# Relative-bias tables read from short rows in reverse key order, the second table built after the first MLP, and two weight splits moved to VectorE

## The chip, the cores and the metric

The kernel runs on one core of one Trainium2 chip. The metric is the device time in microseconds of one execution of the whole program. Six instruction streams run side by side: TensorE (PE, with its weight loads shown as PEld), VectorE (DVE), ScalarE (ACT), GpSimd (POOL), and the queues from which transfers are issued; SyncE (SP) does nothing else, ACT and POOL issue some transfers between their computations. Each stream works its instructions in order.

## The reference, cut to what matters

A sequence of 256 tokens with 1024 features goes through a first block of two layers and a second block. All of it is float32; the kernel gets float32 accuracy by splitting each operand into a high part (rounded to the type that TensorE multiplies fast) and the rest, and by adding three products.

```
# first block, layer A: attention with an indexer and a relative bias
score = sum_h w[t,h] * relu(q_idx[t,h] . k_idx[s]) * ...   # top 64 keys of a token are kept
logits[h,t,s] = q[t,h].k[s] / 8 + rel_bias[bucket(s - t)][h]     # 16 heads, 32 buckets
h = h + softmax(logits) @ v @ a_w_o
h = h + relu(rms(h) @ up)**2 @ down                         # MLP 0
# layer B: latent attention, no bias table
h = h + mla(h) @ b_w_o ;  h = h + MLP 1
# second block: mLSTM beside attention in 3 groups of 8 heads
logits[g,h,t,s] = q.k / 8 + rel_bias_2[bucket(t - s)][8 g + h]   # masked outside the group's window
h = merge(...) ; h = h + gated FFN ; out = rms(h) * g
```

A bias depends only on the distance between key and query. For each head it is one row of some 383 numbers, and the 256 x 256 bias of a head is that row, shifted by one place from one query to the next.

## The kernel before, in words

Tokens lie on the 128 partitions in two tiles t = 0 and 1; the residual stream stays on the chip in `hres[0]` and `hres[1]`. Weights are streamed: `wsplit` loads up to four 128-row blocks into a tile `raw` (3 buffers) over SP's queue, ACT makes the high part `whi`, and DVE the rest `wlo` (4 buffers each). A load waits until the split of three loads earlier has read its buffer, and a split waits until TensorE has finished with the weights of four splits earlier.

The program is written with a tile framework that derives the waits and also reorders the instructions of each engine by a cost model of its own; the plans `PLAN_A`, `PLAN_B` and `PLAN_C` only give the order in which the pieces are handed to it. In `PLAN_A` "s" is the indexer's scores of a tile (`scores`), "k" its top-k (`topk`, eight rounds of maximum and replace on DVE, which end in the mask `madd`), "q" the query projection, "t" the transposes of the queries, a star a round of attention steps, and "x" the making of the second bias table.

A bias table is made in two steps. `bias_rows` multiplies a one-hot matrix `oh` (33 x 512, from the constant `c_oh`) by the table `rb` on TensorE into `bt`, ACT copies that to `bts`, and a transfer on ACT's queue writes the rows to `vec` in device memory. Then a second transfer on ACT's queue, device memory to device memory, writes for each head and each of 128 queries the shifted row of 256 keys: `toe_a` (16 heads, 2 MB) and `toe_b` (24 heads, 3 MB). `load_bias` reads four heads at a time from there over SP's queue. In `att_step` one DVE instruction for each head (CUSTOM_DVE_ANT in the profile, line 547) adds bias and logits and takes the maximum; ACT takes the exponential, TensorE transposes the result (`tr`), ACT or DVE copies it (`pT`, a pool of two buffers), and TensorE multiplies by the values into `po`.

The rest `wlo` of the second half of the columns of `a_w_o` and `b_w_o` (four instructions of 128x1024 each) is computed on POOL (`eng=G`), all others on DVE. At the end of MLP 0 the last chunks of the down projection (`dn`) are added to `hres`; layer B then takes sums of squares of `hres` (`sq`, ACT), transposes it (`tr`), splits the result (`bxh`, `bxl`) and multiplies it by `w_dkv` and `b_w_dq`, whose splits carry the gains `gckv` and `gcq`; `low_rank` scales the outcome into `lc`. The tables `tabk` and `tabq` of the rotary embedding are made on DVE from small loads (`rp`, `bgk`, `bgq`).

Of the kernel before, what the change touches and what calls it, by code (L numbers as in the profile page):

```python
# [17 lines left out]
P = 128  # L18
S = 256
# [8 lines left out]
PLAN_A = "s0 k0 q0 q1 t00 t01 s1 * t10 k1 *4 x t11 **"  # L28
# [7 lines left out]
def constants():  # L36
# [31 lines left out]
    c["c_oh"] = oh  # L68
# [21 lines left out]
def block_kernel(ctx: ExitStack, tc: tile.TileContext, a, out: bass.AP):  # L90
# [55 lines left out]
    nc.sync.dma_start(hres[0], a["x"][0, 0:P, :])  # L146
    nc.sync.dma_start(ident, a["c_sq"][:, 0:128])

# [88 lines left out]
    def wsplit(w, k0, kk, c0, n, gain=None, eng=None):  # L237
# [22 lines left out]
    def wparts(w, KT, c0, n, k0=0, gain=None, eng=None):  # L260
        return [(g, min(4, KT - g), wsplit(w, k0 + g, min(4, KT - g), c0, n, gain, eng)) for g in range(0, KT, 4)]
# [20 lines left out]
    def dense_by_tile(jobs, engs=(None, None), holds=(None, None)):  # L282

        parts = []
        for (_, KT, w, c0, n, gain, _), e, hold in zip(jobs, engs, holds):
            with behind(hold):
                parts.append(wparts(w, KT, c0, n, gain=gain, eng=e))
# [87 lines left out]
    def mlp(i):  # L375
# [36 lines left out]
        last([6, 7])  # L412

# [899 lines left out]
```

## Time and profile before

| | |
|---|---|
| three timed runs | 1178.22, 1170.07, 1175.39 us (median 1175.39) |
| the profiled execution | 1170.38 us, of which the span of the trace is 1168.6 us |
| busy in the span | PE 97%, weight loads 85%, DVE 58%, ACT 52%, POOL 9% |
| moved by transfers | 197.16 MB, 169 GB/s in the mean |
| chain that ended last | PE 87%, DVE 4%, DMA 3%, ACT 2%, POOL 2% |

The profiled execution is 5.0 us below the median of the timed runs and 0.3 us above the fastest. The busy shares are means over stages that differ: TensorE has hardly any idle time in the MLPs and the second block, and most of it in the two attention layers of the first block and at both ends.

### The profile page before, as it was taken

The numbers are of one execution on the slowest core, as the hardware profiler recorded it, in microseconds if no ns is written. First come the engines' busy times: TensorE is split into PE (matmuls) and PEld (weight loads), VectorE is DVE, ScalarE is ACT, GpSimd is POOL, SyncE is SP. The second block draws the span as 40 slices with busy tenths as digits, with TensorE's granted clock in tenths as the row PEclk, the third lists the DMA queues.
The fourth block names the chain that finished last, engine by engine and source line by source line (L and its number), as shares of the span: only waits on it lengthen the run. The fifth ranks groups of instructions, "written<-read, shape, count | busy, mean of one in ns | idle before, by whom it ended". The sixth has DMA issues, their size and how long they took to land.

```text
span 1168.6 us, 17282 instructions
## 1 busy us (share of the span) xinstructions
PE 1128.3 (97%) x6912; PEld 994.9 (85%) x6912; DVE 680.9 (58%) x1182; ACT 613.0 (52%) x1070; POOL 109.6 (9%) x128
## 2 busy tenths in 40 slices
PE   7979899999997999999999999999999999999997
PEld 6747799899886888998889999889888878999996
DVE  5694654544578666445446885655474556544544
ACT  7564555544577556455546574464564435443443
POOL 1250000000039400000000000010000030000000
PEclk9999999999999999999999999999999999999999
DMA  8954455555355226555626644553544544546541
GB/s 276 303 154 92 144 182 179 198 199 164 102 150 173 91 73 216 198 181 185 210 88 244 212 154 145 201 177 132 180 158 144 169 138 162 195 166 216 199 137 62
DMA packets 110339, 197.16 MB, mean 169 GB/s; under 512 B 6580, under 2 KB 28044, under 8 KB 110260
## 3 DMA queue, kind: packets, MB, share of 16 engines
q1 hardware_dynamic: 103704, 186.90, 47.7%
q10 hardware_dynamic: 5516, 5.64, 2.1%
q0 software_dynamic: 1040, 3.54, 1.1%
q8 instruction: 54, 0.88, 0.3%
q14 instruction: 25, 0.20, 0.1%
HBM read 194.93 MB, written 6.37 MB: 172 GB/s over the span
## 4 chain that ended last, share of the span: by engine, by line
PE 87%; DVE 4%; DMA 3%; ACT 2%; POOL 2%; issue 1%; SPq 0%; ACTq 0%; POOLq 0%; DVEq 0%
PE acc L269 8%; PE acc L270 8%; PE acc L272 8%; PE dn L356 7%; PE dn L355 7%; PE dn L358 7%; PE up L304 5%; PE up L307 5%; PE up L305 5%; PE tr L164 3%; PE po L503 3%; PE lg L479 2%; PE qk L305 2%; PE qk L304 2%; PE qk L307 2%; DMA toe_a<-vec 2%
## 5 line engine op out<-in xcount | busy, mean ns | idle before, releaser
L250 DVE TENSOR_TENSOR wlo<-raw,whi 128x1024 fp32r<-128x1024 f32 (+3 forms) x332 | 376.7, 1176 | 210.7 <-ACT whi L247 210.1
L247 ACT ACTIVATE whi<-raw 128x1024 fp32r<-128x1024 f32 (+3 forms) x340 | 323.2, 1008 | 212.4 <-PE dn L358 84.9
L157 POOL TENSOR_TENSOR rr<-rv,mhalf 128x1 f32<-128x1 f32 (+2 forms) x42 | 40.4, 961 | 796.3 <-DVE rv L155 794.0
L304 PE MATMUL up<-mxh,whi 128*128 128x256 f32 x448 | 111.5, 282 | 0.0
L305 PE MATMUL up<-mxl,whi 128*128 128x256 f32 x448 | 111.2, 280 | 0.0
L356 PE MATMUL dn<-wlo,uh 128*128 128x512 f32 x256 | 100.6, 394 | 0.0
L355 PE MATMUL dn<-whi,uh 128*128 128x512 f32 x256 | 100.2, 393 | 0.0
L304 PEld LDWEIGHTS up<-mxh,whi 128*128 128x128 f32 x448 | 84.3, 188 | 0.7
L305 PEld LDWEIGHTS up<-mxl,whi 128*128 128x128 f32 x448 | 84.3, 188 | 0.7
L269 PE MATMUL acc<-whi,cxh 128*128 128x512 f32 (+1 forms) x192 | 74.6, 390 | 0.0
L270 PE MATMUL acc<-wlo,cxh 128*128 128x512 f32 (+1 forms) x192 | 72.4, 378 | 0.0
L307 PE MATMUL up<-mxh,wlo 128*128 128x256 f32 x448 | 71.2, 281 | 0.0
L358 PE MATMUL dn<-whi,ul 128*128 128x512 f32 x256 | 69.6, 394 | 0.0
L307 PEld LDWEIGHTS up<-mxh,wlo 128*128 128x128 f32 x448 | 60.6, 188 | 0.0
L358 PEld LDWEIGHTS dn<-whi,ul 128*128 128x128 f32 x256 | 48.1, 188 | 11.2
L355 PEld LDWEIGHTS dn<-whi,uh 128*128 128x128 f32 x256 | 48.1, 188 | 10.6
L356 PEld LDWEIGHTS dn<-wlo,uh 128*128 128x128 f32 x256 | 48.1, 188 | 10.6
L272 PE MATMUL acc<-whi,cxl 128*128 128x512 f32 (+1 forms) x192 | 50.5, 382 | 0.0
L168 DVE TENSOR_TENSOR ul<-sq,uh 128x512 fp32r<-128x512 f32 x28 | 19.4, 692 | 51.2 <-ACT uh L168 50.8
L304 PE MATMUL qk<-cxh,whi 128*128 128x256 f32 x192 | 49.1, 287 | 0.0
L305 PE MATMUL qk<-cxl,whi 128*128 128x256 f32 x192 | 48.3, 282 | 0.0
L487 ACT ACTIVATE lg<-lg,nx 128x128 f32<-128x128 f32 (+1 forms) x80 | 35.5, 446 | 17.3 <-DVE nx L547 16.7
(414 smaller groups left out, 2461.6 us busy)
## 6 DMA issues: line engine op xcount, KB each, us to landing
raw<-in_w_in SPq DMA_DIRECT2D x38, 1024.0 KB
raw<-in_mlp_w_up SPq DMA_DIRECT2D x32, 1024.0 KB
raw<-in_mlp_w_down SPq DMA_DIRECT2D x32, 1024.0 KB
raw<-in_w_gate SPq DMA_DIRECT2D x10, 1024.0 KB
raw<-in_w_up SPq DMA_DIRECT2D x10, 1024.0 KB
raw<-in_w_down SPq DMA_DIRECT2D x10, 1024.0 KB
raw<-in_w_in SPq DMA_DIRECT2D x6, 688.0 KB
raw<-in_a_w_in SPq DMA_DIRECT2D x4, 1024.0 KB
```

Of the source, the lines that this page charges most:

```text
L157: G.tensor_tensor(r[:, :n], v[:, :n], mhalf[:, :n], op=OP.pow)
L247: A.activation(hi[:, c], raw[:, c], AF.Copy)
L250: (eng or V).tensor_tensor(lo[:, c], raw[:, c], hi[:, c].bitcast(F32), op=OP.subtract)
L269: PE.matmul(o, s0, wh[:, k, :], start=(g + k == 0), stop=False)
L270: PE.matmul(o, s0, wl[:, k, :], start=False, stop=False)
L272: PE.matmul(o, xs(xl, g + k, t), wh[:, k, :], start=False, stop=(g + k == KT - 1))
L304: PE.matmul(o, s0, xh[(g + k) // 4][:, (g + k) % 4, :], start=(g + k == 0), stop=False)
L305: PE.matmul(o, s0, xl[(g + k) // 4][:, (g + k) % 4, :], start=False, stop=False)
L307: PE.matmul(o, wl[:, k, col:col + P], xh[(g + k) // 4][:, (g + k) % 4, :], start=False, stop=(g + k == KT - 1))
L355: PE.matmul(ps, s0, wh[:, k, :], start=(c == 0 and k == 0), stop=False)
L356: PE.matmul(ps, s0, wl[:, k, :], start=False, stop=False)
L358: PE.matmul(ps, xs(u[1], k, t), wh[:, k, :], start=False, stop=(c == nc_ - 1 and k == kt - 1))
```

## The change

There are five edits. (1) The large tables `toe_a` and `toe_b` go away: the one-hot constant is stored with its key axis reversed, so that `load_bias` can read the shifted rows straight from `vec` (partition step +1, key step +1) and `att_step` reads the loaded tile backwards (`Sk - 1::-1`). (2) The second table is built at the end of MLP 0 (`biases_2`) instead of inside layer A ("x" leaves `PLAN_A`). (3) The one-hot tiles are loaded over SP's queue instead of ACT's, and take the buffers of `pT`; `bts` takes those of `sq`, and `bt` those of the transposes. (4) The first tile of `x` is loaded in two halves and the first weight group in four blocks. (5) The splits of `a_w_o` and `b_w_o` are all on DVE.

```diff
-PLAN_A = "s0 k0 q0 q1 t00 t01 s1 * t10 k1 *4 x t11 **"
+PLAN_A = "s0 k0 q0 q1 t00 t01 s1 * t10 k1 *4 t11 **"
...
-    c["c_oh"] = oh
+    c["c_oh"] = np.concatenate([oh[:, :, 382::-1], np.zeros((33, 4, 129), np.float32)], axis=2)
...
-    nc.sync.dma_start(hres[0], a["x"][0, 0:P, :])
+    nc.sync.dma_start(hres[0][:, 0:512], a["x"][0, 0:P, 0:512])
     nc.sync.dma_start(ident, a["c_sq"][:, 0:128])
+    nc.sync.dma_start(hres[0][:, 512:1024], a["x"][0, 0:P, 512:1024])
...
+        if by_k:
+            for k in range(kk):
+                nc.sync.dma_start(raw[:, k * n:(k + 1) * n], w[(k0 + k) * P:(k0 + k + 1) * P, c0:c0 + n])
...
-                (eng or V).tensor_tensor(lo[:, c], raw[:, c], hi[:, c].bitcast(F32), op=OP.subtract)
+                V.tensor_tensor(lo[:, c], raw[:, c], hi[:, c].bitcast(F32), op=OP.subtract)
...
         last([6, 7])
+        if i == 0:
+            biases_2()
...
-    def bias_rows(coef, K, M, ohs, dst):
-
-        vec = dr.tile([M * len(ohs), 512], F32, name=nm("vec"))
-        for g, (oh, c0) in enumerate(ohs):
-            ps = lgp("bt")
-            PE.matmul(ps[:M, :], coef[:K, c0:c0 + M], oh[:K, :], start=True, stop=True)
-            sb = t2("bts")
-            A.activation(sb[:M, :], ps[:M, :], AF.Copy)
-            nc.scalar.dma_start(vec[g * M:(g + 1) * M, :], sb[:M, :])
-        nh = M * len(ohs)
-        v0 = vec[0:1, 0:1]
-        nc.scalar.dma_start(dst, bass.AP(tensor=v0.tensor, offset=v0.offset + 127,
-                                         ap=[[512, nh], [-1, P], [1, S]]))
...
+    def bias_rows(which, K, M, c0, vec):
+
+        oh = tpt("oh")
+        nc.sync.dma_start(oh[:33, :], a["c_oh"][:, which, :])
+        ps = trp("bt")
+        PE.matmul(ps[:M, :], rb[:K, c0:c0 + M], oh[:K, :], start=True, stop=True)
+        sb = tj("bts")
+        A.activation(sb[:M, :], ps[:M, :], AF.Copy)
+        nc.scalar.dma_start(vec, sb[:M, :])
...
+    def biases_2():
+        for g in range(3):
+            bias_rows(1 + g, 33, 8, 16 + 8 * g, vec_b[g])
...
-        b = quad(t4("bias"), S)
-        nc.sync.dma_start(b, toe[h0:h0 + 4, :, :].rearrange("h p s -> p h s"))
+    def load_bias(vec, h0):
+
+        b = quad(t4("bias"), S)
+        v0 = vec[h0:h0 + 1, 0:1]
+        nc.sync.dma_start(b, bass.AP(tensor=v0.tensor, offset=v0.offset, ap=[[1, P], [512, 4], [1, S]]))
...
-            bs_ = bias(c // 2)[:, 2 * (c % 2):2 * (c % 2) + 2, 2 * P - Sk:]
+            bs_ = bias(c // 2)[:, 2 * (c % 2):2 * (c % 2) + 2, Sk - 1::-1]
...
-        out_proj(oT, a["a_w_o"][0], eng=G)
+        out_proj(oT, a["a_w_o"][0])
...
-        out_proj(oT, a["b_w_o"][0], eng=G)
+        out_proj(oT, a["b_w_o"][0])
```

The diff alone doesn't tell where the framework's scheduler puts the moved instructions. Four pieces of the order follow; a number behind a name is a buffer's, and differs between the two programs.

ACT in layer A, behind the splits of the last query weights (`whi` with `gca`), before the change: `qiT` are the indexer's transposed queries, `rl` its scores behind the relu, `q` the projected queries.

```order
L255 ACTIVATE whi_554<-raw_553,gca 128x512 x4
L615 ACTIVATE qiT_373<-tr_368 128x512
L459 DMA oh_768<-in_c_oh 33x512
L632 ACTIVATE rl_399<-lg_397 128x256
L459 DMA oh_770<-in_c_oh 33x512
L632 ACTIVATE rl_405<-lg_403 128x256
L459 DMA oh_772<-in_c_oh 33x512
L660 ACTIVATE q_496<-acc_471,rr_131 128x512
L661 ACTIVATE q_496<-acc_471,rr_131 128x512
L632 ACTIVATE rl_411<-lg_409 128x256
L247 ACTIVATE whi_1045<-raw_1044 128x1024 x2
```

The same place after the change.

```order
L260 ACTIVATE whi_558<-raw_557,gca 128x512 x4
L612 ACTIVATE qiT_377<-tr_372 128x512
L629 ACTIVATE rl_403<-lg_401 128x256
L629 ACTIVATE rl_409<-lg_407 128x256
L657 ACTIVATE q_500<-acc_475,rr_137 128x512
L658 ACTIVATE q_500<-acc_475,rr_137 128x512
L252 ACTIVATE whi_1026<-raw_1025 128x1024 x2
L629 ACTIVATE rl_415<-lg_413 128x256
L657 ACTIVATE q_535<-acc_510,rr_162 128x512
L658 ACTIVATE q_535<-acc_510,rr_162 128x512
L252 ACTIVATE whi_1034<-raw_1033 128x1024 x2
```

The three loads of one-hot tiles, for the second table, stood between the score copies on ACT; they are gone from there.

DVE in layer A, the end of the first top-k (`m`, `scr`) up to the first attention step (ISA, which reads `bias`), before the change.

```order
L647 MATCH_REPLACE scr_385<-m_98_439,scr_385 128x128
L645 MAX m_99_442<-scr_385 128x8
L647 MATCH_REPLACE scr_385<-m_99_442,scr_385 128x128
L650 TENSOR_SCALAR madd_445<-scr_385 128x128
L636 SCALAR_TENSOR_TENSOR scr_386<-rl_649,w_67_375,chmask_303 128x256
L636 SCALAR_TENSOR_TENSOR scr_386<-rl_649,w_67_375,scr_386 128x256
L663 TENSOR_REDUCE qss_628<-q_625 128x8
L155 TENSOR_SCALAR rv_630<-qss_628 128x8
L636 SCALAR_TENSOR_TENSOR scr_386<-rl_655,w_67_375,scr_386 128x256 x2
L547 ISA lg_671,nx_394<-lg_672,bias_377 128x128
```

The same place after the change, from the seventh of the eight rounds.

```order
L644 MATCH_REPLACE scr_389<-m_97_443,scr_389 128x128
L633 SCALAR_TENSOR_TENSOR scr_390<-rl_653,w_66_379,scr_390 128x256
L255 TENSOR_TENSOR wlo_1051<-raw_1049,whi_1050 128x1024
L156 TENSOR_SCALAR rv_634<-qss_632 128x8
L642 MAX m_98_446<-scr_389 128x8
L255 TENSOR_TENSOR wlo_1051<-raw_1049,whi_1050 128x1024
L633 SCALAR_TENSOR_TENSOR scr_390<-rl_659,w_66_379,scr_390 128x256
L644 MATCH_REPLACE scr_389<-m_98_446,scr_389 128x128
L633 SCALAR_TENSOR_TENSOR scr_390<-rl_659,w_66_379,scr_390 128x256
L647 TENSOR_SCALAR madd_449<-scr_389 128x128
L633 SCALAR_TENSOR_TENSOR scr_390<-rl_665,w_66_379,scr_390 128x256
L544 ISA lg_675,nx_398<-lg_676,bias_381 128x128
```

Two of the four splits of the second half of `a_w_o` (`wlo`) now stand ahead of `madd` here, the other two a few rows further up, and four of the eight steps of the second tile's scores (`scr_390`) have moved ahead of `madd`, with a fifth right behind it; before, none stood ahead of it.

SP's queue at the handover from MLP 0 to layer B, before the change.

```order
L242 DMA raw_2846<-in_w_dkv 128x4x288
L242 DMA raw_2858<-in_w_dkv 128x4x288
L437 DMA rp_2748<-in_c_rope 128x2x64
L437 DMA bgk<-in_k_norm 128x32
L437 DMA bgq<-in_b_q_norm 128x32
L437 DMA gcol<-in_k_norm 64x1
L437 DMA gcol<-in_b_q_norm 64x1
L242 DMA raw_2870<-in_b_w_dq 128x4x384
L242 DMA raw_2882<-in_b_w_dq 128x4x384
L242 DMA raw_3116<-in_w_ukv 128x2x512
L744 DMA QT_2828<-in_c_mq 2x1024
```

The same place after the change.

```order
L247 DMA raw_2848<-in_w_dkv 128x4x288
L247 DMA raw_2860<-in_w_dkv 128x4x288
L247 DMA raw_2872<-in_b_w_dq 128x4x384
L247 DMA raw_2884<-in_b_w_dq 128x4x384
L247 DMA raw_3118<-in_w_ukv 128x2x512
L428 DMA oh_2743<-in_c_oh 33x512
L441 DMA rp_2750<-in_c_rope 128x2x64
L441 DMA bgk<-in_k_norm 128x32
L441 DMA bgq<-in_b_q_norm 128x32
L441 DMA gcol<-in_k_norm 64x1
L441 DMA gcol<-in_b_q_norm 64x1
```

The third one-hot tile is loaded here, because the pool of `pT` has two buffers and the first one is free only when TensorE has multiplied the first `oh`; the small loads for `tabk` and `tabq` stand behind it in the queue. The two earlier `oh` loads stand among MLP 0's first weights.

ACT at the same handover, before the change.

```order
L174 ACTIVATE sq_2779,ss_446_2778<-h_70 128x512
L174 ACTIVATE sq_2781,ss_446_2778<-h_70 128x512
L255 ACTIVATE whi_2847<-raw_2846,gckv 128x288 x4
L255 ACTIVATE whi_2859<-raw_2858,gckv 128x288 x4
L174 ACTIVATE sq_2804,ss_454_2803<-h_71 128x512
L168 ACTIVATE bxh_2774<-tr_2789 128x4x128
L174 ACTIVATE sq_2806,ss_454_2803<-h_71 128x512
L168 ACTIVATE bxh_2775<-tr_2796 128x4x128
L255 ACTIVATE whi_2871<-raw_2870,gcq 128x384 x4
L255 ACTIVATE whi_2883<-raw_2882,gcq 128x384 x4
```

The same place after the change.

```order
L260 ACTIVATE whi_2849<-raw_2848,gckv 128x288 x4
L260 ACTIVATE whi_2861<-raw_2860,gckv 128x288 x4
L432 ACTIVATE bts_2733<-bt_2731 8x512
L433 DMA vec_b_78<-bts_2733 8x512
L432 ACTIVATE bts_2740<-bt_2738 8x512
L433 DMA vec_b_79<-bts_2740 8x512
L432 ACTIVATE bts_2747<-bt_2745 8x512
L169 ACTIVATE bxh_2776<-tr_2791 128x4x128
L433 DMA vec_b_80<-bts_2747 8x512
L175 ACTIVATE sq_2781,ss_444_2780<-h_70 128x512
L169 ACTIVATE bxh_2777<-tr_2798 128x4x128
L260 ACTIVATE whi_2873<-raw_2872,gcq 128x384 x4
```

Three copies `bts` and three writes now stand in front of the first `bxh`, and three of the four sums of squares (`sq`), all of which stood ahead of the splits with `gcq`, have gone behind those splits, outside these rows; on TensorE the three `bt` products stand between the last `dn` and the first `tr` of layer B, which is not shown.

## Rows read from the trace of the kernel before

**Rows 1.** The page's busy times, with shares of the span and instruction counts.

```profile
PE 1128.3 (97%) x6912; PEld 994.9 (85%) x6912; DVE 680.9 (58%) x1182; ACT 613.0 (52%) x1070; POOL 109.6 (9%) x128
```

**Rows 2.** Busy time by stretch, then granted clock, transfer share and GB/s.

```profile
core 0: us, PE busy (x) PEld busy (x) DVE busy (x) ACT busy (x) POOL busy (x), PEclk, DMA share, GB/s
...
60.00:70.00 10.00, 4.68 (x20) 2.31 (x18) 9.69 (x17) 6.25 (x10) 9.89 (x6) 1.00 0.42 132
70.00:80.00 10.00, 9.41 (x39) 5.26 (x40) 9.90 (x42) 6.88 (x26) 5.07 (x4) 0.83 0.60 205
...
360.00:380.00 20.00, 15.47 (x97) 13.05 (x96) 18.77 (x34) 15.43 (x42) 19.09 (x24) 1.00 0.33 106
380.00:400.00 20.00, 17.67 (x118) 16.28 (x118) 14.91 (x36) 13.55 (x37) 13.27 (x17) 0.91 0.40 132
```

**Rows 3.** The chain of waits up to 80 us: start, length, what.

```profile
2.06 7.63 DMA raw<-in_a_w_in
...
22.34 5.08 DMA vec<-bts
...
27.43 17.75 DMA toe_a<-vec
```

**Rows 4.** Timeline of ACT: start, length, instruction, then idle time before it and releaser.

```profile
4.67 0.63 ACT L174 ACTIVATE sq<-h 128x512 f32<-128x512 f32 x1 [2.65 <-DMA h<-in_x]
...
9.78 2.04 ACT L255 ACTIVATE whi<-raw,gca 128x356 fp32r<-128x356 f32 x4 [2.64 <-DMA raw<-in_a_w_in]
...
45.64 0.38 ACT L632 ACTIVATE rl<-lg 128x256 f32<-128x256 f32 x1 [6.08 <-DMA toe_a<-vec]
```

**Rows 5.** Timeline of DVE in layer A's scores, top-k and first attention steps.

```profile
46.05 0.35 DVE L636 SCALAR_TENSOR_TENSOR scr<-rl,w,chmask 128x128 f32<-128x128 f32 x1 [4.66 <-ACT rl L632]
...
49.18 1.23 DVE L250 TENSOR_TENSOR wlo<-raw,whi 128x1024 fp32r<-128x1024 f32 x1
...
61.88 1.30 DVE L650 TENSOR_SCALAR madd<-scr 128x128 bf16<-128x128 f32 x1
...
64.42 2.46 DVE L636 SCALAR_TENSOR_TENSOR scr<-rl,w,scr 128x256 f32<-128x256 f32 x1
...
69.93 0.28 DVE L547 CUSTOM_DVE_ANT_0 lg<-lg,bias 128x128 f32<-128x128 f32 x1
...
70.35 0.48 DVE L636 SCALAR_TENSOR_TENSOR scr<-rl,w,scr 128x256 f32<-128x256 f32 x1
...
71.17 2.42 DVE L636 SCALAR_TENSOR_TENSOR scr<-rl,w,scr 128x256 f32<-128x256 f32 x1
```

**Rows 6.** Timeline of PE: attention logits, the second table, the output projection.

```profile
70.58 1.19 PE L479 MATMUL lg<-KT,qT 128*128 128x256 f32 x2 [2.14 <-DVE nx L547]
...
74.24 1.02 PE L422 MATMUL bt<-oh,rb 33*8 33x512 f32 x2
...
85.94 0.50 PE L269 MATMUL acc<-whi,aoh 128*128 128x512 f32 x1
```

**Rows 7.** Timeline at the handover to layer B, engine by engine.

```profile
296.46 0.46 SPq L437 DMA_DIRECT2D bgk<-in_k_norm  x1
...
299.80 0.19 DVE L723 TENSOR_TENSOR tabk<-rp,bgk 128x32 f32<-128x32 f32 x1 [1.34 <-DMA bgk<-in_k_norm]
...
305.31 0.63 ACT L174 ACTIVATE sq<-h 128x512 f32<-128x512 f32 x1 [7.57 <-DVE h L312]
...
316.01 1.04 PE L164 MATMUL tr<-ident,h 128*128 128x128 f32 x8
...
318.23 4.16 ACT L255 ACTIVATE whi<-raw,gcq 128x384 fp32r<-128x384 f32 x8
...
325.76 0.48 DVE L762 SCALAR_TENSOR_TENSOR lc<-acc,lr,gain 128x256 f32<-128x256 f32 x1
```

**Rows 8.** Timeline of DVE and POOL in layer B's attention.

```profile
374.72 2.03 DVE L812 TENSOR_SCALAR scq<-rr 128x4 f32<-128x4 f32 x1
376.66 2.38 DVE L856 TENSOR_TENSOR nb<-mx,scq 128x2 f32<-128x2 f32 x1
...
374.34 4.69 POOL L250 TENSOR_TENSOR wlo<-raw,whi 128x1024 fp32r<-128x1024 f32 x2
```

More of the change, by code (lines that the diff above doesn't have):

```diff
@@ L235, in xs, with wsplit @@
         return x[k // 4][:, k % 4, t * P:(t + 1) * P]
-    def wsplit(w, k0, kk, c0, n, gain=None, eng=None):
+    def wsplit(w, k0, kk, c0, n, gain=None, by_k=False):
         raw = wp.tile([P, 2048], F32, tag="raw", name=nm("raw"), bufs=NRAW)
@@ L258, in wsplit, with wparts @@
         return v(hi), v(lo)
-    def wparts(w, KT, c0, n, k0=0, gain=None, eng=None):
-        return [(g, min(4, KT - g), wsplit(w, k0 + g, min(4, KT - g), c0, n, gain, eng)) for g in range(0, KT, 4)]
+    def wparts(w, KT, c0, n, k0=0, gain=None, by_k=False):
+        return [(g, min(4, KT - g), wsplit(w, k0 + g, min(4, KT - g), c0, n, gain, by_k and g == 0))
+                for g in range(0, KT, 4)]
     def mm_tok(o, x, t, parts, KT):
@@ L280, in dense, with dense_by_tile @@
                 evac(t, ci, ps[:, :n])
-    def dense_by_tile(jobs, engs=(None, None), holds=(None, None)):
+    def dense_by_tile(jobs, holds=(None, None)):
         parts = []
-        for (_, KT, w, c0, n, gain, _), e, hold in zip(jobs, engs, holds):
+        for (_, KT, w, c0, n, gain, _), hold in zip(jobs, holds):
             with behind(hold):
-                parts.append(wparts(w, KT, c0, n, gain=gain, eng=e))
+                parts.append(wparts(w, KT, c0, n, gain=gain))
         for t in range(2):
@@ L292, in dense_by_tile, with out_proj @@
                 evac(t, ps[:, :n])
-    def out_proj(x, w, scale=None, eng=None):
+    def out_proj(x, w, scale=None):
         dense_by_tile([(x, 8, w, 512 * ci, 512, None, lambda t, ps, ci=ci: add_res(t, ci, ps, scale))
-                       for ci in range(2)], [None, eng])
+                       for ci in range(2)])
     def mm_feat(o, x, parts, KT, col):
@@ L412, in mlp @@
         last([6, 7])
+        if i == 0:
+            biases_2()
     def len_u(u):
         return u[0][0].shape[1]
-    def bias_rows(coef, K, M, ohs, dst):
-        vec = dr.tile([M * len(ohs), 512], F32, name=nm("vec"))
-        for g, (oh, c0) in enumerate(ohs):
-            ps = lgp("bt")
-            PE.matmul(ps[:M, :], coef[:K, c0:c0 + M], oh[:K, :], start=True, stop=True)
-            sb = t2("bts")
-            A.activation(sb[:M, :], ps[:M, :], AF.Copy)
-            nc.scalar.dma_start(vec[g * M:(g + 1) * M, :], sb[:M, :])
-        nh = M * len(ohs)
-        v0 = vec[0:1, 0:1]
-        nc.scalar.dma_start(dst, bass.AP(tensor=v0.tensor, offset=v0.offset + 127,
-                                         ap=[[512, nh], [-1, P], [1, S]]))
-    toe_a = dr.tile([16, P, S], F32, name="toe_a")
-    toe_b = dr.tile([24, P, S], F32, name="toe_b")
+    def bias_rows(which, K, M, c0, vec):
[6 more added lines that the diff above has]
+        nc.scalar.dma_start(vec, sb[:M, :])
+    vec_a = dr.tile([16, 512], F32, name="vec_a")
+    vec_b = [dr.tile([8, 512], F32, name=f"vec_b{g}") for g in range(3)]
     rb = cp.tile([33, 40], F32, name="rb")
@@ L448, in load_consts @@
         return chmask
-    def toeplitz(which):
-        if which == 0:
-            oh = t2("oh")
-            nc.scalar.dma_start(oh[:33, :], a["c_oh"][:, 0, :])
-            bias_rows(rb, 32, 16, [(oh, 0)], toe_a)
-        else:
-            ohs = []
-            for g in range(3):
-                oh = t2("oh")
-                nc.scalar.dma_start(oh[:33, :], a["c_oh"][:, 1 + g, :])
-                ohs.append((oh, 16 + 8 * g))
-            bias_rows(rb, 33, 8, ohs, toe_b)
+    def biases_2():
+        for g in range(3):
+            bias_rows(1 + g, 33, 8, 16 + 8 * g, vec_b[g])
     def quad(tl, Sk):
@@ L576, in layer_a @@
         V.tensor_copy(gcol, gp[:, :8])
-        wkv = [wparts(w, 8, *kvc[0], gain=gcol)]
+        wkv = [wparts(w, 8, *kvc[0], gain=gcol, by_k=True)]
         nc.sync.dma_start(hres[1], a["x"][0, P:2 * P, :])
@@ L622, in layer_a @@
         sco = [None, None]
-        bias = [load_bias(toe_a, 4 * i) for i in range(4)]
+        bias = [load_bias(vec_a, 4 * i) for i in range(4)]
         ring = [t4("scr").rearrange("p (i s) -> p i s", i=4) for _ in range(2)]
@@ L1169, in get_bias @@
         def get_bias(gi):
-            gbias[gi] = [load_bias(toe_b, gi * 8 + 4 * q) for q in range(2)]
+            gbias[gi] = [load_bias(vec_b[gi], 4 * q) for q in range(2)]
         for gi in range(3):
```

10 lines of the change are left out of this document (5 added, 5 removed).

## The prediction

> **What bounds the kernel now.** I read the page's busy times first: TensorE is busy for 97% of the span [rows 1], so a change can only win where TensorE idles or runs slowly. The stretches show where: between 60 and 80 us it is busy for 14.1 of 20 us, with a granted clock of 0.83 in the second half, and between 360 and 400 us for 33.1 of 40, with 0.91 in the second half [rows 2]. In the first of these DVE is busy for 19.6 of 20 us; in the second, POOL is busy for 19.1 of 20 and then DVE for 18.8 [rows 2]. So the two attention layers of the first block are bound by DVE and POOL, everything between them by TensorE. Next I read the chain of waits: up to 45 us it goes through the landing of the first weights (7.63 us), the write of the bias rows (5.08) and the write of the large table (17.75) [rows 3]. The timelines tell who is hit by the last: ACT idles for 6.08 us in front of its first score copy `rl`, because the one-hot load in front of it on its queue waits for that write [rows 4], and DVE idles for 4.66 us behind it [rows 5].
>
> **The first loads in pieces.** ACT starts to square `x` at 4.67 us, when all of it is there, and to split the first weights at 9.78, after 2.64 us of idle time for the load [rows 4]. Cut in four, the first quarter can land at the earliest a quarter of the way between these two, at about 5.9 us, which would let the splits start up to 3.8 us sooner. But ACT is kept busy after that by work whose own loads come later over the same queue, and four more issues stand in front of them. Bounds 0 and 3.5 us; I take 2.0, nearer to the middle, because ACT is the engine in front of TensorE here and one of its entries (the one-hot load) goes too.
>
> **The large table's write.** Removing it takes away ACT's wait. The bound from above is 6.08 us [rows 4], from DVE's side 4.66 [rows 5]. Some of it stays, because TensorE now runs most of the rest of a query product ahead of these logits; I take 4.1. With the 2.0 from the start DVE's scores begin at 46.05 - 6.1 = 39.95 us.
>
> What is late next is DVE itself. From its first score step to the end of `madd` it worked for 61.88 + 1.30 - 46.05 = 17.1 us [rows 5]. Now four splits stand in there as well, at 1.23 us each = 4.9, and four wide score steps, at 0.48 each = 1.9; the 1.30 of `madd`, taken while POOL ran its splits, falls to about 0.4 (a step of twice that width takes 0.48 [rows 5]). 17.1 + 4.9 + 1.9 - 0.9 = 23.0 us, so `madd` ends at 62.95, just where it ended before (63.18). The earlier start is spent on the moved work. The gain comes behind `madd`: the first attention step began 6.75 us after it (at 69.93 [rows 5]), with score steps between that took up to 2.46 us instead of 0.48. Now one step of 0.48 is left there: first attention step at 63.4, a gain of 6.5. From there to the output projection DVE has no idle time (9.90 of 10 us [rows 2]), and the step of 2.42 us at 71.17 shrinks by 1.9 [rows 5]. That makes 8.4 by the start of the output projection (85.94 [rows 6]), from where TensorE is the bound; I take **8.5**, with one score step less in that stretch. Bounds: 5 (nothing from the start, 3 us from the wait) and 10.5 (3.5 from the start).
>
> TensorE's three `bt` products (1.02 us a pair of instructions [rows 6]) leave this stretch at no gain of their own: DVE's work covers them. TensorE's logits run at half clock at 70.58 (two take 1.19 us [rows 6]) after the idle stretch before; it will idle as long in front of `madd` now, so I leave that as it is.
>
> **Splits off POOL in layer B.** While POOL ran two splits for 4.69 us, two tiny DVE instructions took 2.03 and 2.38 us [rows 8]; without POOL they'd take some 0.15 each, as their kind does elsewhere, and the second pair of splits, near 388 us, shows the same once more at a little less. I count 4.1 + 3.2 = 7.3 us of holds against four splits on DVE at 1.23 [rows 5], 4.9: a gain of 2.4, and a little for POOL's own chain: **2.5**. Bounds 0 and 5.
>
> The Trainium skill, page "SBUF — State Buffer", section "Who interferes with whom", says that a DVE instruction with two SBUF inputs contends with a GpSimd instruction that reads SBUF, that the port is held for the whole instruction, and that the issue order decides who waits. The trace agrees with it on one side, DVE held behind POOL [rows 8]. By that rule the moved splits, which read two SBUF tiles each, hold POOL in their turn, and then the gain of 2.5 shrinks or becomes a loss; the first rival is this case, worked out there from rows.
>
> **The second table at the end of MLP 0.** This is the cost. Before, TensorE turned from the last `dn` to `tr` at 316.01 and ACT began the `gcq` splits at 318.23 [rows 7]. Now three `bt` stand between. Two have their one-hot tiles since layer A (their loads wait on SP's queue for the last readers of `pT`, some microseconds before the fourth weight load of MLP 0 could go anyway, so they cost nothing; without that, a late weight load). The third tile's buffer is the first one's: its load can start only when the first `bt` is done, at 317.0. A small load took 3.3 us from issue to first use (296.46 to 299.80 [rows 7]): 320.3. Third `bt`, 1.0 us, then its copy on ACT, some 0.6 like other ACT copies of that width, and only then `bxh`: 5.3 us later than before, the `gcq` splits start at about 323.5 instead of 318.23. The transfers for `tabk` and `tabq` stand behind that load on SP's queue, and DVE takes them before `bxl`; they land within the same delay. Behind the splits ACT now has three squares at 0.63 us and their read-outs (two ahead of `bxh` of the second tile, one ahead of the evacuation) that used to be done while `dn` ran [rows 7]: about 2.0 more for `lc`, which comes at 333 instead of 325.76. Later TensorE waits give back some 0.5 to 1, and a stretch with so little TensorE work may cost some clock, as between 70 and 80 us. I take a loss of **7.0**. Bounds 4.5 (a load in 2.3 us, squares half hidden) and 10.5 (the row write at 5.08 us [rows 3] holding the buffer of the third copy, and 2 us of clock).
>
> **Edits that I cost at nothing.** The transfers that go (2 MB and 3 MB written and read) only shared the queues with weights that TensorE didn't wait for at that time. `load_bias` moves as many bytes in as many pieces of 1 KB as before. The backward read of the bias tile on DVE has no row in this trace: I take it at the forward price (0.28 us for 128 wide [rows 5]), which it equals unless a step back costs more than one forward; a gain is excluded, since the same elements are read. Above, the bound is twice the price, a rival below.
>
> **How the numbers follow.** 8.5 + 2.5 - 7.0 = 4.0 us faster. Against the profiled execution, 1170.4, that is 1166.4; the timed runs' median stands 5.0 above that execution, so the prediction for the median is 1175.4 - 4.0 = **1171**. Its own range is 1164 to 1178. A change of under 1% (11.8 us) is about what a measurement of this kernel can't tell from none; so I forecast no change that can be told, a little on the fast side. Chance 0.60.
>
> **Rivals.**
> - *DVE takes over, slower* (0.13). TensorE's order gives the logits hardly earlier than the table's wait did, so that scores begin only 2.0 us sooner; then `madd` ends at 67.0, and 8.5 becomes 4.4. In layer B each of the four splits on DVE holds a POOL step on the path for its 1.23 us: 2.5 - 4.9 = -2.4. Sum 4.4 - 2.4 - 7.0 = -5.0: 1180. It decides once the two layers together lose 4 of their 11 us. For it: DVE at 9.7 to 9.9 of 10 us [rows 2]; against it: POOL had idle time behind each split.
> - *Shifted reads are slow* (0.10). The write of 17.75 us read the rows in just this shifted way [rows 3]; if the reading was what took so long, the bias loads take it over, on SP's queue in front of the third load of `a_w_o`, whose splits now stand ahead of `madd`. About 4.5 us late: -0.5 in sum, 1176. Against it: that transfer also wrote 2 MB and shared the engines with weights.
> - *Backward reads at half speed* (0.07). 16 narrow steps stand where DVE is the bound: 16 x 0.28 = 4.5; another 64, most of them twice as wide, stand where TensorE is, and a quarter of their some 29 us shows: 7. Sum 4.0 - 11.5 = -7.5: 1183.
> - *The handover costs its least, and both layers give their most* (0.10): 10.5 + 5 - 4.5 = 11.0 faster, 1164.
>
> The range that leaves out no more than 2 in 10 is 1162 to 1180: it takes in the forecast, the fast rival, the slow reads and the edge of the first rival. Faster by over 1% (below 1163.6) 0.08, slower by over 1% (above 1187) 0.04, within it 0.88.
>
> **What would show it.** In the new profile: ACT's first `rl` without a wait for a transfer, at 39 to 42 us; the first attention step on DVE at 62 to 65; the output projection's first product at 76 to 80; no DVE instruction of two microseconds in either attention layer; between the last `dn` and layer B's first `tr` an idle gap on TensorE of 2 to 4 us that ends with the third one-hot load; `lc` 6 to 9 us later after the last `dn` than the 9.7 us of before; and DVE's bias step at 0.28 us as now. The prediction is wrong if scores don't start earlier, if the bias loads run into the third load of `a_w_o`, or if the handover costs under 4 or over 11 us.

## The result

The changed kernel takes 1167.43 us in the median of nine runs (1163.82 to 1168.29), the kernel before 1176.64 (1170.07 to 1178.64): a ratio of 0.9924, 95% interval 0.9909 to 0.9939. That is 9 us faster, where 4 were forecast (1171). The profiled executions differ by 3.0 us only (1170.38 and 1167.43); where the other 6 are, the experiment on the kernel before tells.

The page's busy times of the changed kernel answer to [rows 1], and its stretches to [rows 2]:

```profile
PE 1130.8 (97%) x6912; PEld 998.9 (86%) x6912; DVE 676.4 (58%) x1190; ACT 613.0 (53%) x1070; POOL 95.9 (8%) x120
```

```profile
60.00:70.00 10.00, 8.05 (x44) 5.54 (x44) 9.97 (x54) 8.40 (x37) 4.35 (x3) 1.00 0.67 223
70.00:80.00 10.00, 8.43 (x50) 6.68 (x49) 7.69 (x25) 1.77 (x5) 0.00 (x0) 1.00 0.01 2
...
120.00:140.00 20.00, 17.55 (x86) 14.18 (x85) 13.49 (x18) 12.50 (x19) 1.63 (x1) 0.91 0.58 199
...
300.00:320.00 20.00, 18.81 (x92) 14.49 (x91) 11.72 (x36) 12.34 (x29) 0.56 (x1) 0.91 0.40 114
...
360.00:380.00 20.00, 18.49 (x121) 17.03 (x122) 18.46 (x48) 18.63 (x48) 15.65 (x25) 0.91 0.49 159
380.00:400.00 20.00, 17.95 (x91) 15.85 (x89) 9.45 (x23) 7.75 (x23) 6.91 (x9) 0.74 0.24 79
```

TensorE fills layer A's gap better (8.05 and 8.43 of 10 us for 4.68 and 9.41, of which the second at a clock of 0.83). But four of these stretches now have a granted clock under 1.00. Of the same six in the kernel before, two had: at 120 to 140 and at 300 to 320 us its clock was 1.00. Timeline of layer A in the changed kernel (ACT, DVE, PE), to set against [rows 4 to 6]:

```profile
39.47 0.76 ACT L629 ACTIVATE rl<-lg 128x256 f32<-128x256 f32 x2
...
39.88 0.35 DVE L633 SCALAR_TENSOR_TENSOR scr<-rl,w,chmask 128x128 f32<-128x128 f32 x1 [2.03 <-ACT rl L629]
...
62.49 0.21 DVE L647 TENSOR_SCALAR madd<-scr 128x128 bf16<-128x128 f32 x1
...
63.07 0.28 DVE L544 CUSTOM_DVE_ANT_0 lg<-lg,bias 128x128 f32<-128x128 f32 x1
...
75.47 0.50 PE L275 MATMUL acc<-whi,aoh 128*128 128x512 f32 x1
```

ACT's first `rl` waits for no transfer any more; the first attention step comes 6.9 us sooner, the output projection 10.5. Timeline of the handover to layer B (PE, ACT, DVE, SP), against [rows 7] (`dn` are MLP 0's last down products, `bt` the three products of the second table, `tr` the transposes for layer B):

```profile
305.23 1.09 PE L364 MATMUL dn<-whi,ul 128*128 128x512 f32 x4
306.25 1.88 PE L430 MATMUL bt<-oh,rb 33*8 33x512 f32 x4
309.32 1.02 PE L430 MATMUL bt<-oh,rb 33*8 33x512 f32 x2 [1.19 <-DMA oh<-in_c_oh]
310.26 1.86 PE L165 MATMUL tr<-ident,h 128*128 128x128 f32 x8
...
312.83 4.15 ACT L260 ACTIVATE whi<-raw,gcq 128x384 fp32r<-128x384 f32 x8
316.88 0.62 ACT L175 ACTIVATE sq<-h 128x512 f32<-128x512 f32 x1
...
322.40 0.48 DVE L759 SCALAR_TENSOR_TENSOR lc<-acc,lr,gain 128x256 f32<-128x256 f32 x1
...
307.30 0.32 SPq L428 DMA_DIRECT2D oh<-in_c_oh  x1
```

The third `bt` waits 1.19 us for the third one-hot load, the eight `tr` behind it take 1.86 us instead of 1.04 (half clock), and `lc` comes 16.1 us behind the last `dn` (306.32) instead of 9.6 (316.17 to 325.76). One view more, the groups of DVE's bias step, by shape (busy time, mean ns of one), in the kernel before and in the changed one, which reads the bias tile backwards:

```profile
L547 DVE CUSTOM_DVE_ANT_0 lg<-lg,bias 128x256 f32<-128x256 f32 x40 | 15.1, 419 | 8.4 <-PE lg L479 6.5 <-PE lg L481 1.7
L547 DVE CUSTOM_DVE_ANT_0 lg<-lg,bias 128x128 f32<-128x128 f32 x40 | 9.9, 285 | 5.9 <-DMA bias<-toe_b 4.4 <-PE lg L479 1.5
```

```profile
L544 DVE CUSTOM_DVE_ANT_0 lg<-lg,bias 128x256 f32<-128x256 f32 x40 | 15.0, 420 | 10.2 <-PE lg L476 6.5 <-PE lg L478 2.4 <-PE tr L165 1.1
L544 DVE CUSTOM_DVE_ANT_0 lg<-lg,bias 128x128 f32<-128x128 f32 x40 | 9.6, 283 | 5.4 <-DMA bias<-vec_b 3.9 <-PE lg L476 1.5
```

Backwards or forwards, it takes the same.

### The profile page after: what moved, and what is told of

It reads as the page before. It is cut to its first block, busy times and chain, and to the rows that moved or that the text cites. A ratio compares the mean times of both kernels' runs of the same rounds, so it can differ in the third digit from the quotient of the medians.

```text
span 1165.6 us, 17291 instructions
## 1 busy us (share of the span) xinstructions
PE 1130.8 (97%) x6912; PEld 998.9 (86%) x6912; DVE 676.4 (58%) x1190; ACT 613.0 (53%) x1070; POOL 95.9 (8%) x120
## 4 chain that ended last, share of the span: by engine, by line
PE 67%; DVE 1%; issue 1%; POOL 1%; ACT 1%; POOLq 0%; DVEq 0%
PE acc L275 7%; PE acc L276 7%; PE acc L278 7%; PE dn L361 4%; PE dn L362 4%; PE dn L364 4%; PE tr L165 3%; PE up L310 2%; PE up L313 2%; PE up L311 2%; PE po L500 2%; PE qk L311 2%; PE qk L310 2%; PE qk L313 2%; PE fg L311 1%; PE fp L311 1%
## 5 line engine op out<-in xcount | busy, mean ns | idle before, releaser
L255 DVE TENSOR_TENSOR wlo<-raw,whi 128x1024 fp32r<-128x1024 f32 (+3 forms) x340 | 387.0, 1179 | 209.9 <-ACT whi L252 209.2
```

What stands on the lines that cost most here:

```text
L255: V.tensor_tensor(lo[:, c], raw[:, c], hi[:, c].bitcast(F32), op=OP.subtract)
```

## The experiments

Diffs are against the changed kernel unless they say otherwise. Ratios are to the kernel before, in the runs beside the experiment.

**The kernel before, twice more** (no edit).

> The kernel before, unchanged, with a second profile. The profiled execution of before (1170.38 us) is 6 us under the median of its nine timed runs (1176.6), while that of the changed kernel sits on its median. Theory: the difference is TensorE's granted clock; in the first profile of before half clock was granted for 8.9 us in all (mean clock 0.996), and a usual execution has 20 us or more of it (mean clock near 0.990, span near 1175). Rival: the clock is 0.995 or above again and some 5 us of waiting stand elsewhere, at the end or in a transfer.

This was inconclusive: ten runs gave 1171.88 us in the median (1170.02 to 1177.89; ratio 0.9983, 0.9964 to 1.0003), but the profiled execution again had a high clock (1171.84 us, mean clock 0.994). A third execution was profiled:

> The kernel before, unchanged, once more, for a profile of one of its executions near 1176 us (of 38 timed ones 29 lie at 1174 to 1178 with a mean granted clock of 0.984 to 0.991, 9 at 1170 to 1172 with 0.994 to 0.996; both profiles so far are of the second kind). Theory (the two kinds differ by TensorE's clock alone): the landmarks up to layer B stand where they did within 1 us, and the 5 us more lie in stretches of half clock, which sum to 25 us or more instead of 9 to 12. Rival: a wait of some us that the other profiles don't have stands somewhere.

This execution took 1175.75 us. Its stretches, and its timeline of PE:

```profile
60.00:70.00 10.00, 4.45 (x18) 2.02 (x18) 9.76 (x18) 6.94 (x11) 9.89 (x6) 0.96 0.43 138
70.00:80.00 10.00, 9.98 (x24) 4.32 (x25) 7.35 (x27) 5.70 (x24) 4.51 (x4) 0.50 0.55 183
80.00:90.00 10.00, 10.00 (x37) 6.38 (x36) 6.65 (x31) 4.11 (x15) 0.00 (x0) 0.69 0.05 15
```

```profile
74.13 1.87 PE L422 MATMUL bt<-oh,rb 33*8 33x512 f32 x2
...
91.48 0.50 PE L269 MATMUL acc<-whi,aoh 128*128 128x512 f32 x1
```

Up to the first attention step all stands where it did (69.37 us, [rows 5]). Then TensorE stays at half clock from 69.1 to 86.2 us: 17.1 us of it instead of 3.4, a pair of `bt` takes 1.87 us instead of 1.02 [rows 6], and the output projection starts 5.5 us later than in the first profile. From there on the two run alike within 0.1 us a stage. No wait was added; it is the clock. Why it fell for so much longer in this execution, no run shows. In 61 executions of the kernel before that show their clock, 12 had 0.993 to 0.996 and took 1170.0 to 1172.8 us, and 49 had 0.984 to 0.991 and took 1173.5 to 1180.4. The profile that the prediction was read from (0.996) is of the first kind; of the second kind one execution was profiled. The theory's total was a little too high: half clock sums to 20.5 us up to TensorE's last product, 22.8 over the span, and not 25.

**The second table in layer A again**, with x for `biases_2`, which leaves MLP 0.

```diff
-PLAN_A = "s0 k0 q0 q1 t00 t01 s1 * t10 k1 *4 t11 **"
+PLAN_A = "s0 k0 q0 q1 t00 t01 s1 * t10 k1 *4 x t11 **"
```

> The changed kernel with the second table built in layer A again, at the old place of the plan, everything else as changed. Theory (the handover is paid for by the move: TensorE's first tr of layer B 4.1 us after the last dn and lc 16.2 us after it, where it was 9.7): the handover is back at 9.5 to 10.5 us from the last dn to lc, layer A loses at most 2 us by the three bt products, because DVE is the bound there, and the whole is 1161 to 1164 us (1167.4 less 6, plus up to 2). Rival (the table costs as much wherever it stands, since its products and copies sit on the same engines): layer A gives back 4 us or more and the whole stays within 1166 to 1169.

Measured 1166.72 us (ratio 0.9919, 0.9895 to 0.9943): no change that can be told from the changed kernel. The handover went back to 9.6 us as expected, but layer A gave all of it back. PE in layer A:

```profile
73.15 1.02 PE L428 MATMUL bt<-oh,rb 33*8 33x512 f32 x2 [0.59 <-DMA oh<-in_c_oh]
74.65 1.01 PE L428 MATMUL bt<-oh,rb 33*8 33x512 f32 x2 [0.48 <-DMA oh<-in_c_oh]
76.19 1.79 PE L428 MATMUL bt<-oh,rb 33*8 33x512 f32 x2 [0.53 <-DMA oh<-in_c_oh]
...
82.72 0.78 PE L275 MATMUL acc<-whi,aoh 128*128 128x512 f32 x1
```

The theory that DVE's work covers the three products fell: the output projection came 7.3 us later. But each product waited for its load here, and 6.8 us of half clock followed, so this run doesn't tell the place from the buffers. Another one does, with the table at the same place and the tiles in the pool that the kernel before used:

```diff
-        oh = tpt("oh")
+        oh = t2("oh") if which else tpt("oh")
```

> The second table in layer A as in the second experiment, but its one-hot tiles take buffers of the pool of 128x512 work tiles, as in the kernel before, instead of the two of pT. Theory (there the products waited for loads that waited for pT's buffers, 1.6 us of idle time that brought two stretches of half clock with it): no idle time in front of a bt, the output projection's first product at 76 to 78.5 us instead of 82.72, the whole 1160 to 1163. Rival (three products and three copies in that stretch cost what they cost): the output projection at 80 us or later, the whole 1165 to 1168.

```profile
71.14 1.02 PE L428 MATMUL bt<-oh,rb 33*8 33x512 f32 x2
...
78.33 0.50 PE L275 MATMUL acc<-whi,aoh 128*128 128x512 f32 x1
```

No product waits for a load, and the output projection starts at 78.33: 4.4 us of the 7.3 go with the waits for buffers (and with the 6.8 us of half clock behind them), 2.9 remain with the products and copies. The time, 1164.21 us (1158.98 to 1166.89; ratio 0.9897, 0.9875 to 0.9919), is 1 us above what was expected and 3.2 us below the changed kernel's, though the intervals overlap.

**The w_o splits back on POOL**, in both layers (`a_w_o` likewise), and in layer B alone.

```diff
-                V.tensor_tensor(lo[:, c], raw[:, c], hi[:, c].bitcast(F32), op=OP.subtract)
+                (eng or V).tensor_tensor(lo[:, c], raw[:, c], hi[:, c].bitcast(F32), op=OP.subtract)
...
-        out_proj(oT, a["b_w_o"][0])
+        out_proj(oT, a["b_w_o"][0], eng=G)
```

> The changed kernel with the second half of the w_o splits of both layers back on POOL. Theory (the table's write was what held layer A, the splits are worth little): in layer A four splits of 1.23 us leave DVE and two or three holds of about 2 us come back, the first attention step comes at 63 to 67 us instead of 63.07; in layer B the holds come back and POOL's steps go free; the whole is 1167 to 1171. Rival (POOL's hold on DVE was most of the gain): the first attention step comes at 68 or later and the whole is 1173 to 1177.

Measured 1170.59 us (ratio 0.9953, 0.9939 to 0.9967). DVE in layer A:

```profile
57.03 1.06 DVE L647 TENSOR_SCALAR madd<-scr 128x128 bf16<-128x128 f32 x1
58.02 2.60 DVE L633 SCALAR_TENSOR_TENSOR scr<-rl,w,scr 128x256 f32<-128x256 f32 x1
...
63.68 0.28 DVE L544 CUSTOM_DVE_ANT_0 lg<-lg,bias 128x128 f32<-128x128 f32 x1
...
64.92 2.42 DVE L633 SCALAR_TENSOR_TENSOR scr<-rl,w,scr 128x256 f32<-128x256 f32 x1
```

`madd` comes 5.5 us sooner without the splits, and holds of 2.60 and 2.42 us behind it, with others, give that back: the first attention step comes 0.6 us later than in the changed kernel. From there to the output projection (78.57) it takes 14.9 us instead of 12.4, with 3.4 us of half clock that the changed kernel's trace hasn't there. Theory held.

> The changed kernel with the second half of the w_o splits back on POOL in layer B alone. Theory (in layer B DVE holds POOL now as POOL held DVE before, so the move is worth 0 to 1.5 us there, and the 3.2 us that both layers' splits are worth together lie mostly in layer A): from the transposes of lc to the output projection 71.5 to 73 us, where it is 71.6; the whole 1167.4 to 1169. Rival (layer B holds the 2.5 us that the prediction gave it): the whole 1169.5 to 1171.

Measured 1169.67 us (ratio 0.9945, 0.9928 to 0.9963). The rival's time came: layer B alone is worth 2.2 us by the medians, though the interval still overlaps the changed kernel's, and from the transposes of `lc` to the output projection it took 73.7 us instead of 71.6. Its holds on DVE, while POOL ran two splits, and then, in the changed kernel, the other way round (POOL and DVE; the two POOL steps by themselves, with their shortest, median and longest time in ns; and one step of that kind with no split beside it):

```profile
373.16 2.14 DVE L809 TENSOR_SCALAR scq<-rr 128x4 f32<-128x4 f32 x1
...
375.22 2.38 DVE L853 TENSOR_TENSOR nb<-mx,scq 128x2 f32<-128x2 f32 x1
...
372.89 4.68 POOL L255 TENSOR_TENSOR wlo<-raw,whi 128x1024 fp32r<-128x1024 f32 x2
```

```profile
380.76 3.79 POOL L732 TENSOR_TENSOR qb<-qb,tabq 128x128 f32<-128x128 f32 x2
...
L732 POOL TENSOR_TENSOR qb<-qb,tabq x2: 460/1918/3377, 380.8 to 381.2; 128x128 f32<-128x128 f32 x2
...
381.58 1.19 DVE L255 TENSOR_TENSOR wlo<-raw,whi 128x1024 fp32r<-128x1024 f32 x1
...
348.63 0.45 POOL L732 TENSOR_TENSOR qb<-qb,tabq 128x128 f32<-128x128 f32 x1
```

Of two POOL steps the first took its usual 0.46 us, the second 3.38, beside two of DVE's splits. The Trainium skill, page "SBUF — State Buffer", section "Who interferes with whom", has it that whichever of the two was issued first holds the port and the other waits; these rows agree that each side can hold the other. For the order they agree only where POOL holds DVE: the POOL step that was held is recorded as begun at 381.17, 0.41 us ahead of DVE's split.

**The large tables gone alone.** Against the kernel before: the short-table reads and new pools stay, the one-hot loads are on SP's queue, the table is in layer A, the first loads are whole, and the splits are on POOL.

> The kernel before with the large tables gone alone: bias rows read straight from the short table with reversed keys, the one-hot tiles and small tiles in their new pools and on SP's queue, but the second table in layer A, the first loads whole and the second halves of the w_o splits on POOL as before. Theory (ACT's and DVE's wait for the table's write is the first thing that goes): DVE's first score step comes 4 to 5 us sooner than before (at 41 to 42 us), half or more of that reaches the output projection; the whole is 1170 to 1174 against 1176.6. Rival (DVE and POOL hold each other in that stretch whatever the table does): the scores start sooner but the output projection's first product moves by less than 1.5 us, and the whole is 1175 to 1178.

```profile
40.82 0.35 DVE L630 SCALAR_TENSOR_TENSOR scr<-rl,w,chmask 128x128 f32<-128x128 f32 x1 [0.32 <-ACT rl L626]
...
89.39 0.58 PE L274 MATMUL acc<-whi,aoh 128*128 128x512 f32 x1
```

Scores start 4.7 to 5.7 us sooner than in the three profiles of before. The loads through `pT`'s buffers then cost here too (0.73, 0.30 and 0.28 us in front of the three `bt`, 6.8 us of half clock behind them), and the output projection comes only 2.1 us before that of the usual execution of before (91.48), and later than in the other two (85.94 and 86.41). The time is 1173.59 us (ratio 0.9982, 0.9970 to 0.9994), within the theory's range, though less than half of the gain reached the output projection.

**Four places for the second table, or buffers for it.** First, the third one-hot tile from another pool:

```diff
-        oh = tpt("oh")
+        oh = t2("oh") if which == 3 else tpt("oh")
```

> The changed kernel with the third one-hot tile of the second table in another pool (that of 128x512 work tiles), so that its load doesn't wait for the first bt product. Theory (part of the handover's loss is that wait): no idle time in front of the third bt, the first tr of layer B 3.1 to 3.4 us behind the last dn instead of 3.9, tabk's small loads land before bxh is there, lc 14 to 15 us behind the last dn instead of 16.1, the whole 1165 to 1166.5. Rival (the three products, their copies and the squares that went behind the splits are the whole loss): lc still comes 15.5 us or more behind the last dn, the whole is 1167 to 1168.

```profile
307.26 2.74 PE L430 MATMUL bt<-oh,rb 33*8 33x512 f32 x6
...
321.80 0.48 DVE L759 SCALAR_TENSOR_TENSOR lc<-acc,lr,gain 128x256 f32<-128x256 f32 x1
```

The wait is gone and `lc` comes 14.5 us behind the last `dn` (307.33): 1.6 us less. The time, 1166.63 us (ratio 0.9921, 0.9899 to 0.9942), can't be told from the changed kernel's. So the wait for the load, with the half clock that began behind it at 310.5, is a quarter of the handover's loss.

Then the table inside MLP 0, behind `up(c)` for c = 2, 3 and 4:

```diff
+            if i == 0 and c < 5:
+                bias_rows(c - 1, 33, 8, 8 * c, vec_b[c - 2])
...
-            biases_2()
```

> The changed kernel with the second table made inside MLP 0, one product at a time between the up and down projections of its third to fifth chunk, so that the loads are early and no engine waits. Theory (at the end of MLP 0 the table costs 6.4 us, of which 3.1 is three products on TensorE and the rest is waiting): from the last dn to lc 9.5 to 10 us again, MLP 0 longer by 3.1 us, the whole 1163 to 1165. Rival (as the second table in layer A showed, it costs its 6 us wherever it stands): the whole is 1166.5 to 1168.5.

```profile
L430 PE MATMUL bt<-oh,rb 33*8 33x512 f32 x6 | 3.1, 591 | 0.0
```

```profile
320.21 0.48 DVE L759 SCALAR_TENSOR_TENSOR lc<-acc,lr,gain 128x256 f32<-128x256 f32 x1
```

The group of `bt` shows no idle time in front of it, and `lc` comes 9.6 us behind the last `dn` (310.62). MLP 0, from the first `mxh` product (121.64), takes 189.0 us instead of 185.1: 3.1 of products and 0.8 around them. At 1162.57 us (1159.93 to 1165.54; ratio 0.9887, 0.9862 to 0.9911) this has the lowest median of the study, though the next two (1164.21 and 1164.65) can't be told from it; three of its six runs, at 1160 us, had a clock of 0.997 to 0.998.

Handed in all at once, behind `up(1)` of MLP 0:

```diff
+        if i == 0:
+            biases_2()
         step, last = down_acc(a["mlp_w_down"][i], us, 8)
```

> The changed kernel with the second table handed in after the first up projections of MLP 0, where TensorE idles 2.2 us for the second tile's hn and then gets half clock. Theory: the products lie in the idle time at least in part, from the first mxh product to the last dn 1 to 3 us longer, from the last dn to lc 9.5 to 10 us; the whole 1161.5 to 1164.5. Rival (the third one-hot load waits for the first product there too, as it did in layer A): TensorE stands for a transfer in front of a bt and half clock follows; the whole 1166 to 1168.

1164.65 us (ratio 0.9897, 0.9874 to 0.9919). The scheduler put the products at 134.64, 138.39 and 141.53 us, behind the idle time and not in it, so that they cost what they cost inside MLP 0 (188.9 us); nothing waited for a load. Handed in as the first thing in MLP 0, ahead of its norm, they stand in front of it:

```diff
+        if i == 0:
+            biases_2()
         g = gain_row(a["mlp_norm"][i])
```

> The changed kernel with the second table handed in at the start of MLP 0, ahead of its norm, so that one product stands in layer A's output projection and two directly in front of the transposes of the second hn, where TensorE idled 2.2 us and then ran at half clock. Theory: one product costs 1.0 us, the two in the gap nothing, the half clock behind the gap stays or goes; from the last dn to lc 9.5 to 10 us; the whole 1160 to 1163. Rival (the three loads in front of an MLP weight on SP's queue, or ACT's copies in front of the norm, delay the start of MLP 0): from the first mxh product to the last dn 187 us or more, the whole 1164 to 1167.

1168.95 us (ratio 0.9932, 0.9913 to 0.9952): slower than inside MLP 0, beyond the rival's 1167. ACT (a copy, then the first square) and PE:

```profile
122.29 0.59 ACT L432 ACTIVATE bts<-bt 8x512 f32<-8x512 f32 x1 [6.16 <-PE bt L430]
...
126.81 0.63 ACT L175 ACTIVATE sq<-h 128x512 f32<-128x512 f32 x1 [2.93 <-DMA vec_b<-bts]
...
130.11 1.94 PE L165 MATMUL tr<-ident,hn 128*128 128x128 f32 x8 [7.00 <-DVE hn L193]
```

The two products do stand ahead of the gap, but the gap grows from 2.2 to 7.0 us. `bts` now has `sq`'s two buffers, and the sum of squares that the norm begins with needs one: it waits 2.93 us for a row's write to leave it. The rival's second cause is there too: the copies stand on ACT in front of the norm, and while ACT idles for 6.16 us for the second product, the squares of the first token tile, which begin at 95.30 in the changed kernel, stand behind it.

**The first loads whole**, as before the change.

> The changed kernel with the first tile of x and the first weight group loaded in one transfer each, as before. Theory (the pieces brought the first product from 10.42 to 9.28 us and little else): first product near 10.4, first score step 0.8 to 2 us later than 39.88, the whole 0.5 to 2.5 us slower, 1168 to 1170. Rival (ACT's and TensorE's later work hides it): first score step within 0.5 us of 39.88 and the whole within 1166.9 to 1168.

```profile
10.53 0.66 PE L274 MATMUL acc<-whi,axh 128*128 128x356 f32 x1 [3.27 <-ACT whi L259]
...
41.80 0.35 DVE L632 SCALAR_TENSOR_TENSOR scr<-rl,w,chmask 128x128 f32<-128x128 f32 x1 [0.32 <-ACT rl L628]
```

The first product comes 1.25 us later, the first score step 1.9. The time is 1168.34 us (ratio 0.9930, 0.9908 to 0.9952): 0.9 us slower than the changed kernel, in the trace 1.4 (span 1167.0); as expected in size, though no time of this study can tell it from none.

## Why the prediction was right, and where its sizes were off

The direction and the range held, and the move is under 1%. The range was wide, and the size was off: 9 us for 4. The landmarks add up to the spans, in us (the usual execution of before is the one of 1175.75 us):

| stretch | before, first profile | before, usual | changed | gain to the first | gain to the usual |
|---|---|---|---|---|---|
| to the first `mxh` product | 131.60 | 137.14 | 121.21 | 10.4 | 15.9 |
| to the end of the last `dn` | 184.57 | 184.51 | 185.11 | -0.5 | -0.6 |
| to `lc` | 9.59 | 9.58 | 16.08 | -6.5 | -6.5 |
| to the first `boh` product | 71.57 | 71.49 | 72.11 | -0.5 | -0.6 |
| to the end of the span | 771.27 | 771.28 | 771.09 | 0.2 | 0.2 |
| sum | 1168.6 | 1174.0 | 1165.6 | 3.0 | 8.4 |

By the profiles alone the gain is 3.0 where 4.0 were forecast, and that this is near is luck: layer A gave 1.9 more than its term, layer B 3.0 less, and these two nearly cancel.

*Start and the table's write* (2.0 and 4.1 forecast, first score step at 39.95 us): it came at 39.88; the whole loads give 1.9 of it back, which leaves 4.3 for the write. That division is rough: in the nine traces with the loads in pieces the scores begin at 38.81 to 40.30, and at 40.82 in the run with the large tables gone alone, whose loads are whole. The first attention step, forecast at 63.4, came at 63.07, with `madd` at 62.49 to 62.70 (62.95 forecast): the earlier start was spent on moved work, as said.

*From there to the output projection* the forecast was 1.9 us, by a shrinking hold; it was 3.6 (16.0 to 12.4 us). The step "TensorE's three `bt` products leave this stretch at no gain of their own: DVE's work covers them" failed: with the products back in place and no load to wait for, the stretch takes 16.2 us again. Of these 3.8 us some 1.3 are clock, by the traces with the splits moved and no products there: 12.4 to 12.6 us in three with no half clock in the stretch, 13.6 to 13.7 in four with 3.4 us of it, as that run has. The rest, 2.6, is the products and their copies. Layer A's term was therefore 10.4 in the profile, and not 8.5, at the edge of its bounds. The output projection, at 75.47, came just ahead of the 76 to 80 that were to show it.

*The handover* (7.0 forecast): 6.5. The `gcq` splits begin 6.51 us behind the last `dn` instead of 2.06, 4.5 later where 5.3 was forecast, because the load took 2.0 us from its issue (307.30) to its use (309.32) and not 3.3 (so TensorE's wait for it is 1.19 us, where a gap of 2 to 4 was forecast); the squares behind the splits cost the other 2.0, as forecast. With the table inside MLP 0 all of it goes and 3.9 us come in its place. That is a net gain of 2.6 by the landmarks, 1.9 by the spans, and 4.9 by the medians, where three of the six runs had the higher clock.

*The splits in layer B* (2.5 forecast): 2.2 by the medians of the run that undid them alone. Undone in both layers they make 3.2. How that divides is not settled: by the times layer A has 1.0 of it, but in the trace with both undone the first `mxh` product comes 3.1 us later (124.32) and layer B takes 1.0 longer. The table's row for layer B shows a loss of 0.5 all the same, since the changed kernel's profile has 13.7 us of half clock at 360 to 396 us, the first one of before 3.4. That is more than one execution's chance: at 355 to 400 us the three profiles of before have 3.4 to 6.8 us of it, the eleven others 10.2 to 13.7. Among these is the experiment with the large tables gone alone, with 10.2, where layer B's instructions stand on TensorE, DVE, ACT and POOL in the order of before. In both TensorE waits 1.75 us for a `k` from POOL (at 364.76 before, at 365.27 there), and half clock follows only there. Why is open.

*The offset.* "The timed runs' median stands 5.0 above that execution, so the prediction for the median is 1175.4 - 4.0" is the step that cost most. It took the 5 us for something that stays. In the one usual execution that was profiled they were half clock in layer A behind the idle stretch at 60 to 70 us, in the very place that the change shortens, and there they went with it: the changed kernel's profile lies on its median, and in no trace with the moved splits and no table in layer A was more than 3.4 us of half clock granted up to the output projection. With 5.5 us for that, the three terms as forecast give 1175.4 - 4.0 - 5.5 = 1165.9. Half clock as a whole did not shrink: up to TensorE's last product it is 20.5 us in the changed kernel's profile and in that of the usual execution. But 17.1 of the latter stood in layer A and cost 5.5 us; in the changed kernel none is granted ahead of 129 us.

*The rivals.* DVE did not take over. The shifted reads were not slow: no split of `a_w_o` waited for its load. Backward reading costs nothing (283 and 420 ns, 285 and 419 before). What no part of the prediction had: MLP 0's start loses 0.5 us. TensorE waits there for the second `hn`, before as after, but only after the change does half clock follow (129.6 to 133.0). PE before, then changed:

```profile
139.62 1.29 PE L164 MATMUL tr<-ident,hn 128*128 128x128 f32 x8 [2.23 <-DVE hn L192]
```

```profile
129.21 1.75 PE L165 MATMUL tr<-ident,hn 128*128 128x128 f32 x8 [2.21 <-DVE hn L193]
```

All three profiles of before have this wait (2.18 to 2.23 us) and no half clock behind it; the ten of the changed kernel and its variants that have it (2.16 to 2.23) all have 3.4 us. Why is open here too.

## What to carry to other kernels

Before an offset between a profile and the median is carried along, ask where it lies: here, by one profile, it was clock lost behind an idle stretch, and an edit to that stretch took it too. Small work that is moved out of a busy stage should go into the middle of a stage that TensorE fills, where it costs little more than its own time (3.9 us for 3.1), and not into a seam between stages, where everything behind it on each queue waits (6.5 us); left in layer A, with buffers of its own, it put the output projection off by 2.9 us. When tiles change pools, list who else takes buffers from the new pool: three variants here lost time to such waits (0.28 to 0.73 us in front of each product in layer A, in two runs, and 2.93 us in front of MLP 0's squares).

## What the runs showed of the hardware

The same program, with every instruction in the same order, ran with a mean granted clock of 0.984 to 0.996 on TensorE, and took 1170.0 to 1180.4 us by it. In layer A of the kernel before, half clock began behind a stretch in which TensorE was busy for 4.68 or 4.45 of 10 us, but stayed for 3.4 us in one execution and 17.1 us in another, with TensorE busy for 9.98 of 10 us in the meantime. The same wait of 2.2 us at MLP 0's start was followed by half clock in ten traces of the changed kernel and its variants, and in none of the three of the kernel before. A load of one one-hot tile (33x512) was usable 2.0 us after its issue, and one of two row writes of 16 KB, issued at 122.91 and 123.90, held its buffer until 126.81: 2.9 to 3.9 us.
